# A 2x2 average pool limited by the DMA engines: quarter loads from GpSimd flagged as single packets, and 32 KB store descriptors

## The chip, the cores and the metric

The kernel runs on one core of a Trainium2 chip. The metric is the device time of one execution in microseconds (us). The granted clock was 1.0, and the program used this one core. A time quoted as a median comes from four to seven executions of one kernel.

## The reference, cut to what matters

```python
x = np.random.randn(32, 128, 256, 256).astype(np.float32)   # 1073.7 MB
# kernel_size = 2, stride = 2
output[:, :, i, j] = np.mean(x[:, :, 2*i:2*i+2, 2*j:2*j+2], axis=(2, 3))   # 268.4 MB
```

Every input byte is read once and every output byte written once: 1342.2 MB in all. One output row of 128 values needs two input rows of 256 values. The kernel calls such a pair of rows a unit; there are 4096 units for each of the 128 partitions.

## The kernel before

A tile is 32 units for each partition, which is 64 KB a partition and 8.39 MB in all. There are two buffers for tiles. For each tile, one transfer on SP's queue loads it, VectorE adds twice, ScalarE multiplies by 0.25, and one transfer on ACT's queue stores 16 KB a partition.

```python
sbuf = ctx.enter_context(tc.tile_pool(name="sbuf", bufs=2))
...
for parts in plan:                      # 126 whole tiles, then smaller parts
    in_tile = sbuf.tile([P, G_MAIN, s * w], mybir.dt.float32, name="in_tile")
    ...
        nc.sync.dma_start(out=it, in_=xt)
        nc.vector.tensor_add(out=it[:, :, 0:w], in0=it[:, :, 0:w], in1=...)       # L87
        col_sum = sbuf.tile([P, G_MAIN, w_out], mybir.dt.float32, name="col_sum", bufs=3)
        nc.vector.tensor_add(out=col_sum[:, :g], in0=it[:, :, 0:wu:s], in1=...)   # L96
        nc.scalar.mul(out=col_sum[:, :g], in_=col_sum[:, :g], mul=inv)
        nc.scalar.dma_start(out=ot, in_=col_sum[:, :g])
```

## Time and profile before

The median is 3106.5 us (3106.2 to 3106.7).

| part of a full tile | time |
|---|---|
| VectorE, two additions | 8.69 + 4.42 us |
| ScalarE, one multiplication | 3.62 us |
| from one tile to the next | 24.18 us |
| load issued ahead of the previous tile's landing | about 11 us |

These lines are from the page of the kernel before: the span, the busy times, the data rate in 40 equal slices of the span, and the two DMA queues (packets, MB, share of 16 engines' span).

```profile
span 3104.8 us, 1126 instructions
DVE 1681.4 (54%) x272; ACT 465.8 (15%) x137; POOL 0.2 (0%) x4
DMA  9999999999999999999999999999999999999999
GB/s 418 436 439 425 436 439 425 436 438 429 433 439 430 431 439 434 427 439 435 426 438 436 427 437 436 428 436 437 427 436 437 428 436 437 429 435 437 432 431 396
q1 hardware_dynamic: 19584, 1073.75, 79.8%
q10 hardware_dynamic: 19584, 268.44, 20.2%
```

The DMA engines are full from end to end, and the two queues share them almost exactly as they share the bytes, 4:1. VectorE is busy about half of the time. Its timeline (start, duration, what, and in brackets the idle time before it and what ended that) shows how even the pace is:

```profile
1494.01 8.69 DVE L87 TENSOR_TENSOR in_tile<-in_tile 128x8192 f32<-128x8192 f32 x1 [10.97 <-DMA in_tile<-in_x_dram]
1502.79 4.42 DVE L96 TENSOR_TENSOR col_sum<-in_tile 128x4096 f32<-128x4096 f32 x1
1518.19 8.69 DVE L87 TENSOR_TENSOR in_tile<-in_tile 128x8192 f32<-128x8192 f32 x1 [10.97 <-DMA in_tile<-in_x_dram]
1526.97 4.42 DVE L96 TENSOR_TENSOR col_sum<-in_tile 128x4096 f32<-128x4096 f32 x1
1542.66 8.69 DVE L87 TENSOR_TENSOR in_tile<-in_tile 128x8192 f32<-128x8192 f32 x1 [11.27 <-DMA in_tile<-in_x_dram]
```

Read the bracket as a reserve. With two buffers, the load of tile i+2 is issued when VectorE is done with tile i. VectorE then idles until tile i+1 lands, and that idle time is how far ahead the load of tile i+2 was queued. I call it the lead of the loads: 11 us here.

The trace also holds one record for each DMA descriptor (queue, start, duration, size; the page calls them packets). It does not name the engine, so I assigned records to 16 lanes by matching each start to the end of an earlier record. Lanes can be mixed up when two ends coincide, but the pattern repeats. One lane of the steady state, from that list and not from a view of the profile (L64:2418 is a load descriptor of 64 KB that took 2418 ns, S16 a store descriptor of 16 KB, Ls and Ss are the 4-byte completions):

```
before   L64:2418 S16:611 Ls:9 Ss:9 L64:2418 S16:611 L64:2418 S16:611 L64:2418 S16:611 L64:2418 ...
```

Loads and stores alternate one for one, and nearly every descriptor takes the same time. The two sizes fit 8.6 ns + bytes / 27.2 GB/s. I call this the unobstructed time and what a record takes beyond it its stretch. Over the whole run the stretch is 1.4 us (summed over all records, divided by 16 engines).

### The profile page before, as it was taken

To read this page: it belongs to the slowest core of one execution; us is meant where nothing else is said; L and a number is where in the kernel's file an instruction comes from. 1 tells how busy PE (TensorE), PEld (TensorE's weight loads), DVE (VectorE), ACT (ScalarE), POOL (GpSimd) and SP (SyncE) were. 2 spreads that over 40 slices of the span, in tenths; PEclk is the share of its full clock that TensorE was granted. 3 is DMA by queue.
4 is the path that set the end of the run, shared out by engine and by line. 5 is a ranking of instruction groups with operands and counts; after the bars stand their busy time and mean duration, and the time that the engine had idled before them with its cause. 6 is when DMAs were issued, how large, how long until landed. Compare 5 with 4: busy or idle time off the path is not lost. (4 is left out here: it accounts for less than half of the span.)

```text
span 3104.8 us, 1126 instructions
## 1 busy us (share of the span) xinstructions
DVE 1681.4 (54%) x272; ACT 465.8 (15%) x137; POOL 0.2 (0%) x4
## 2 busy tenths in 40 slices
DVE  4555555555555555555555555555555555555556
ACT  1111111111111111111111111111111111111112
POOL 0000000000000000000000000000000000000000
DMA  9999999999999999999999999999999999999999
GB/s 418 436 439 425 436 439 425 436 438 429 433 439 430 431 439 434 427 439 435 426 438 436 427 437 436 428 436 437 427 436 437 428 436 437 429 435 437 432 431 396
DMA packets 39176, 1342.26 MB, mean 432 GB/s; under 512 B 4352, under 2 KB 4736, under 8 KB 5888
## 3 DMA queue, kind: packets, MB, share of 16 engines
q1 hardware_dynamic: 19584, 1073.75, 79.8%
q10 hardware_dynamic: 19584, 268.44, 20.2%
q14 instruction: 8, 0.07, 0.0%
HBM read 1073.74 MB, written 268.44 MB: 432 GB/s over the span
## 5 line engine op out<-in xcount | busy, mean ns | idle before, releaser
L87 DVE TENSOR_TENSOR in_tile<-in_tile 128x8192 f32<-128x8192 f32 (+4 forms) x136 | 1113.9, 8190 | 1406.7 <-DMA in_tile<-in_x_dram 1406.7
L108 ACT ACTIVATE col_sum<-col_sum 128x4096 f32<-128x4096 f32 (+4 forms) x136 | 464.5, 3415 | 2635.9 <-DVE col_sum L96 2635.9
L96 DVE TENSOR_TENSOR col_sum<-in_tile 128x4096 f32<-128x4096 f32 (+4 forms) x136 | 567.8, 4175 | 13.9 <-DMA out_dram<-col_sum 1.8
L108 ACT ACT_TABLE_LOAD x1 | 1.3, 1283 | 0.7 <-PEq L190 0.7
L190 POOL MEMSET const-bfloat16-1.0<- 128x1 bf16 x1 | 0.1, 102 | 0.0
L190 POOL MEMSET const-uint8-127<- 128x1 uint8 x1 | 0.1, 102 | 0.0
L190 POOL MEMSET const-float32-0.0<- 128x1 f32 x1 | 0.1, 99 | 0.2 <-issue 0.2
L190 POOL MEMSET const-float32-1.0<- 128x1 f32 x1 | 0.1, 99 | 0.0
## 6 DMA issues: line engine op xcount, KB each, us to landing
out_dram<-col_sum ACTq DMA_DIRECT2D x126, 2048.0 KB, 31.6
in_tile<-in_x_dram SPq DMA_DIRECT2D x5, 2048.0 KB, 27.5
in_tile<-in_x_dram SPq DMA_DIRECT2D x1, 4096.0 KB, 25.5
out_dram<-col_sum ACTq DMA_DIRECT2D x5, 512.0 KB, 12.0
in_tile<-in_x_dram SPq DMA_DIRECT2D x126, 35.1
out_dram<-col_sum ACTq DMA_DIRECT2D x1, 1024.0 KB, 12.7
in_tile<-in_x_dram SPq DMA_DIRECT2D x1, 1024.0 KB, 16.2
in_tile<-in_x_dram SPq DMA_DIRECT2D x1, 512.0 KB, 16.9
```

The lines of the kernel that those rows point to most:

```text
L87: nc.vector.tensor_add(out=it[:, :, 0:w], in0=it[:, :, 0:w], in1=it[:, :, di * w : (di + 1) * w],)
L96: nc.vector.tensor_add(out=col_sum[:, :g], in0=it[:, :, 0:wu:s], in1=it[:, :, 1 : wu + 1 : s],)
L108: nc.scalar.mul(out=col_sum[:, :g], in_=col_sum[:, :g], mul=inv)
L190: nc = _bacc.Bacc("TRN2", target_bir_lowering=False, num_devices=1)
```

## The change

The intent is to halve the number of turns between loads and stores while keeping 4:1. Each tile is loaded in four transfers of every fourth partition, in which an engine has two descriptors of 64 KB, flagged to go as a single packet of 128 KB. Two tiles are stored by one transfer with 32 KB descriptors. The loads move to GpSimd's queue, and the tail is cut differently.

```diff
-            nc.sync.dma_start(out=it, in_=xt)
+    def load(it, xt):
+        for q in range(4):
+            nc.gpsimd.dma_start(out=it[q::4], in_=xt[q::4], single_packet=True)
...
+    while left >= 4 * TILE:                       # TILE = 32
+        xt, ot = block(r0, 2 * TILE)              # 64 units a partition, 128 KB in HBM
+        res = out_pool.tile([P, 2 * TILE, w_out], f32, name="res")      # two of these
+        for a in (0, TILE):
+            it = in_pool.tile([P, TILE, 2 * w], f32, name="in_tile")    # two of these
+            load(it, xt[:, a : a + TILE])
+            pool(it, res[:, a : a + TILE])        # the same two additions and the mul
+        nc.scalar.dma_start(out=ot, in_=res)
...
+    # tail: one tile whose store is held back to GpSimd's queue, then parts of 16, 8, 4, 4 units
```

## The prediction

> **What bounds it now.** The DMA engines. The page's slice row shows them 90% busy or more in all 40 slices; its queue table gives loads 79.8% of 16 engines' span and stores 20.2%. 1342.26 MB in a 3104.8 us span is 432 GB/s. VectorE is busy 54%, ScalarE 15%. In the timeline a full tile takes 8.69 + 4.43 us on VectorE and 3.62 us on ScalarE, but tiles follow each other every 24.17 to 24.19 us (a few 24.4 to 24.9), and VectorE idles about 11 us before each, waiting for the load. A tile moves 8.39 MB in and 2.10 MB out: 10.486 MB / 24.175 us = 433.7 GB/s. Loads alone, before the first store, ran at 8.39 MB / 19.32 us = 434.2 GB/s.
>
> The Trainium skill, "DMA: Bandwidth & Descriptors", section "Where 436 GB/s comes from", gives 435.2 GB/s as the SBUF-side ceiling. The trace agrees to 0.4%. At that figure the bytes take 3084 us (estimate), so the kernel has about 22 us to give: some 10 in steady state (128 tiles x 0.08 us), 2 to 4 at the start, some 7 in the tail (the windows view shows 405 GB/s in the last 105 us).
>
> **What the change does.** Loads move from SP's queue to GpSimd's. A 64 KB packet per partition becomes one packet of two partitions (128 KB) per engine; store packets go from 16 to 32 KB. Load packet to store packet stays 4:1, as are the bytes, so alternating packet by packet keeps the queues in balance, with half the switches. If the 0.08 us per tile is paid per packet, half returns: about 5 us. Against that each tile has four load completions instead of one; I allow 0 to 0.1 us a tile, up to 12 us lost. Compute per tile is unchanged. GpSimd has no other work, and a load is issued about 11 us before the previous one lands, which hides slower issue. The start loses about 1 us to GpSimd's issue path. The tail has fewer pieces (16, 8, 4, 4 units, one held-back 2 MB store filling the DMA engines): 0 to 4 us gained; VectorE may wait there for the last 4 MB store to free its buffer.
>
> Nearly all of this is on the critical path, but the sums are tiny: -5 +3 +1 -3, about -4 us.
>
> **Prediction.** 3102 us, range 3089 to 3122. Faster by over 2% would need about 441 GB/s, above anything the trace shows for loads: 3%. Within 2%: 90%. Slower by over 2%: 7%.
>
> **What would show each step.** Right: the DMA row still full, GpSimd's queue near 80% of the engines; load packets per byte about half; VectorE's rhythm 24.1 to 24.25 us per tile, still about 11 us idle per tile for the load; compute busy times unchanged; last 100 us above 405 GB/s. Wrong: a rhythm well over 24.3 us with VectorE waiting longer for loads, or VectorE waiting for stores (two result buffers too few).
>
> **What would make it wrong.** (1) Engine-to-partition assignment. The skill's "SBUF — State Buffer", section "Door 1", maps each group of partitions to one of 16 ports. If 32 partitions taken every fourth are dealt two neighbours to an engine (0 and 4, 8 and 12), two engines meet on one port and loads slow a lot; if each engine keeps its own port's partitions, nothing is lost. No trace here shows which; this is most of the 7%. (2) Completions costing far more on GpSimd's queue. (3) Stores starved behind 128 KB packets, so VectorE waits for a free result buffer. (4) A gain, if overlapping packets let an engine exceed its 27 GB/s.

## More of the kernel before

The experiments ran in five groups, each on a chip of its own with the kernel before beside it. Some comparisons go across groups; the kernel before's medians in the five agree within 0.2 us.

## The result, and the profile after

The changed kernel takes 3203.8 us (median of 4, 3195.2 to 3224.6) against 3106.5 us: slower, ratio 1.032 (1.029 to 1.036). A ratio here is the mean time of one kernel's runs over that of the other's of the same rounds, so it is not quite the ratio of the medians. All four runs counted; their scatter of nearly 1% is new, as the kernel before scatters by 0.02%.

The same lines of the page after the change; its profiled run took 3195.2 us:

```profile
span 3193.5 us, 1676 instructions
DVE 1679.7 (53%) x262; ACT 464.5 (15%) x132; POOL 275.4 (9%) x529
DMA  9999999999999999999999999999999999999999
GB/s 418 426 413 420 420 420 419 419 420 422 417 424 410 417 419 416 424 420 414 421 421 423 420 428 423 419 422 424 424 425 428 424 419 430 417 421 427 422 423 395
q0 software_dynamic: 25296, 1075.87, 80.1%
q10 hardware_dynamic: 9648, 266.34, 19.7%
```

Compute is the same, the engines still look full, and yet they moved 420 GB/s instead of 432 on average. VectorE waits longer for loads. Its waits before and after (engine and line, what it waited for, us in total, times, longest us):

```profile
DVE in_tile L87 <- DMA in_tile<-in_x_dram: 1406.7, 133, 22.7
DVE in_tile L61 <- DMA in_tile<-in_x_dram: 1498.0, 129, 23.6
```

So the transfers themselves take longer. The packet count of the load queue is a first hint: 25296 less the completions (525 transfers x 16 = 8400) leaves 16896 packets of data, as many as one for each partition and transfer, so no data was recorded in 128 KB pieces. VectorE's timeline shows the second hint:

```profile
1495.37 8.69 DVE L61 TENSOR_TENSOR in_tile<-in_tile 128x8192 f32<-128x8192 f32 x1 [17.11 <-DMA in_tile<-in_x_dram]
1504.10 4.42 DVE L62 TENSOR_TENSOR res<-in_tile 128x4096 f32<-128x4096 f32 x1
1514.90 8.69 DVE L61 TENSOR_TENSOR in_tile<-in_tile 128x8192 f32<-128x8192 f32 x1 [6.38 <-DMA in_tile<-in_x_dram]
1523.68 4.43 DVE L62 TENSOR_TENSOR res<-in_tile 128x4096 f32<-128x4096 f32 x1
1545.39 8.69 DVE L61 TENSOR_TENSOR in_tile<-in_tile 128x8192 f32<-128x8192 f32 x1 [17.29 <-DMA in_tile<-in_x_dram]
1554.12 4.43 DVE L62 TENSOR_TENSOR res<-in_tile 128x4096 f32<-128x4096 f32 x1
1564.82 8.69 DVE L61 TENSOR_TENSOR in_tile<-in_tile 128x8192 f32<-128x8192 f32 x1 [6.27 <-DMA in_tile<-in_x_dram]
```

The even rhythm of 24.18 us has become a pair: about 19.4 us, then about 30.4 us, and the lead of the loads falls to 6.3 us in every second tile. A tile in 19.35 us is 434 GB/s of loads alone: no store ran there. A pair takes about 49.7 us where two tiles took 48.36, and 1.35 us x 63 pairs = 85 us, nearly the whole loss.

The lane of one engine shows why there are pairs:

```
after    ... L64:2418 L64:2418 Ls:9 L64:2713 L64:3220 S32:1213 Ls:9 S32:1213 L64:2620 S32:1213 L64:2418
         S32:1213 Ls:9 S32:1213 L64:2418 S32:1213 L64:2418 S32:1213 Ls:9 S32:1213 L64:3185 Ss:9 L64:2418 ...
```

Loads and stores still take turns descriptor by descriptor, now 64 KB against 32 KB, and a load's completion takes a turn too, so that each two load descriptors (128 KB) meet three stores (96 KB). The stores of a pair are used up in some 22 us. Then the store queue is empty for 27 us, until the next pair is done and the stores start again.

The lost time sits at these restarts and ends. The windows view of the changed kernel over one restart (from, to, length, busy time of VectorE, ScalarE and GpSimd, granted clock, DMA share, GB/s) shows loads alone, the restart, the mixed stretch, the end of the stores, and loads alone again:

```profile
1495.40:1511.00 15.60, 13.09 (x2) 2.44 (x1) 2.10 (x4) 1.00 1.00 433
1511.00:1519.00 8.00, 4.10 (x1) 1.17 (x1) 0.00 (x0) 1.00 0.96 360
1519.00:1534.00 15.00, 9.02 (x2) 3.62 (x1) 2.10 (x4) 1.00 1.02 437
1534.00:1543.00 9.00, 0.00 (x0) 0.00 (x0) 0.00 (x0) 1.00 1.04 415
1543.00:1560.00 17.00, 13.12 (x2) 1.42 (x1) 1.16 (x3) 1.00 1.00 432
```

In such short windows a descriptor that straddles an edge blurs the rate, but the records agree: stretched load descriptors of up to 3.4 us lie just before and at the first stores, and a second group lies around the last ones. In between, with stores and loads mixed, descriptors are back at 2418 and 1213 ns. So here 32 KB stores beside 64 KB loads cost nothing once they run.

Summed over all descriptor records (neighbours on an engine overlap by 4 ns, which is taken off), the two spans divide like this:

| us, mean of 16 engines | before | after | difference |
|---|---|---|---|
| unobstructed time of all data descriptors | 3094.3 | 3091.7 | -2.6 |
| stretch | 1.4 | 84.3 | +82.9 |
| rest (start, tail, idle, completions) | 9.1 | 17.5 | +8.4 |
| span | 3104.8 | 3193.5 | +88.7 |

Fewer descriptors did save 2.6 us. Stretch gave it all back thirty times over. Of the 8.4 us in the rest, some 6 us are gaps in mid-run, in which fewer than 16 descriptors were under way. The profiled run was the fastest of the four; the median run lost 97 us.

### The profile page after: what moved, and what is told of

The parts are those of the page before. It is cut to its first block, busy times and chain, and to the rows that moved or that the text cites. A ratio compares the mean times of both kernels' runs of the same rounds, so it can differ in the third digit from the quotient of the medians.

```text
span 3193.5 us, 1676 instructions
## 1 busy us (share of the span) xinstructions
DVE 1679.7 (53%) x262; ACT 464.5 (15%) x132; POOL 275.4 (9%) x529
## 3 DMA queue, kind: packets, MB, share of 16 engines
q0 software_dynamic: 25296, 1075.87, 80.1%
## 4 chain that ended last, share of the span: by engine, by line
DMA 69%; DVE 26%; POOL 3%; issue 1%; DVEq 0%; ACT 0%; ACTq 0%; PEldq 0%
DMA in_tile<-in_x_dram 69%; DVE in_tile L61 17%; DVE res L62 9%; POOL in_tile L58 3%; ACT res L63 0%; DVEq L61 0%; DVEq L62 0%; ACTq L112 0%; PEldq L204 0%
## 5 line engine op out<-in xcount | busy, mean ns | idle before, releaser
L61 DVE TENSOR_TENSOR in_tile<-in_tile 128x8192 f32<-128x8192 f32 (+1 forms) x131 | 1113.1, 8497 | 1498.1 <-DMA in_tile<-in_x_dram 1498.0
L63 ACT ACTIVATE res<-res 128x4096 f32<-128x4096 f32 (+1 forms) x131 | 463.2, 3538 | 2723.0 <-DVE res L62 2722.5
L62 DVE TENSOR_TENSOR res<-in_tile 128x4096 f32<-128x4096 f32 (+1 forms) x131 | 566.7, 4327 | 9.5 <-DMA in_tile<-in_x_dram 1.3
L58 POOL DMA_DIRECT2D in_tile<-in_x_dram x524 | 274.7, 527 | 2902.1 <-DVE res L62 2849.0
```

The lines of the kernel that those rows point to most:

```text
L58: nc.gpsimd.dma_start(out=it[q::4], in_=xt[q::4], single_packet=True)
L62: nc.vector.tensor_add(out=dst, in0=it[:, :, 0:w:2], in1=it[:, :, 1:w:2])
L63: nc.scalar.mul(out=dst, in_=dst, mul=0.25)
```

## The experiments

All kernels gave correct results. Each is the changed kernel with the edit shown (e18 builds on e3), so they share its tail and its paired layout. Each was run four times, with seven runs of before beside it, whose medians were 3106.3 to 3106.4 us. Where an edit has one mul for a pair, the mul for each tile is left out. "Stretch" and "dry" (how long the store queue is empty before a restart) come from the descriptor records of the profiled run. Counted from the last store on any engine to the next first one, "dry" comes out up to 3 us shorter. Stretch is put down to a restart or to the end of the stores, whichever is nearer in time. Losses of about 1% below are clear of the noise: e2's ratio of 1.013 has an interval of 1.011 to 1.015.

**The first four** take the change apart. Theory A was: the mismatch of turns makes the stores stop and go, and each restart costs. Its rivals were GpSimd's loads (B), the 128 KB row pitch in HBM that pairing brings (C), and 32 KB descriptors as such (D).

```diff
 # e1_pool_16k: one store per tile
             pool(it, res[:, a : a + TILE])
-        nc.scalar.dma_start(out=ot, in_=res)
+            nc.scalar.dma_start(out=ot[:, a : a + TILE], in_=res[:, a : a + TILE])
 # e2_sp_32k: the load of before
-        for q in range(4):
-            nc.gpsimd.dma_start(out=it[q::4], in_=xt[q::4], single_packet=True)
+        nc.sync.dma_start(out=it, in_=xt)
 # e3_sp_16k: both of these
 # e4_no_single
-            nc.gpsimd.dma_start(out=it[q::4], in_=xt[q::4], single_packet=True)
+            nc.gpsimd.dma_start(out=it[q::4], in_=xt[q::4])
```

> The changed kernel with one edit: each tile is stored by itself, so store descriptors are 16 KB again. Theory A (stop and go: the engines alternate load and store descriptor by descriptor, 64 KB against 32 KB, so the stores run at twice the share of the bytes, run dry and start again once per pair of tiles, and each stop and start costs the engines about 1.35 us): back to 3095-3110 us, tiles every 24.1-24.3 us, load descriptors at 2418 ns throughout. Theory B (GpSimd's loads: four quarters, their completions or descriptor rings, slow mixed traffic): stays near 3190-3205. Theory C (the 128 KB pitch of the rows in HBM that the pairing of tiles brings): stays near 3190-3205. Theory D (a 32 KB store descriptor is slow in itself): 3095-3110, like A.

> The changed kernel with the loads of before (one transfer of 128 partitions per tile on SP's queue), 32 KB stores kept. A: as slow as the changed kernel, 3180-3210 us, tiles alternating near 19.35 and 30.3 us. B: 3095-3110. C and D: 3180-3210.

> The changed kernel with both undone: SP loads and 16 KB stores, but the paired layout (128 KB pitch) and the new tail kept. A, B, D: 3095-3108 us. C: 3180-3205.

> The changed kernel without the single-packet flag. A: the descriptors were dealt one by one even with the flag, so no change, 3190-3215 us. If the flag itself costs the time (it holds an engine through two descriptors): clearly faster than the changed kernel. If the flag does hold two load descriptors together in part, dropping it makes the alternation worse: over 3215.

| | median us | ratio to before | stretch us | dry us |
|---|---|---|---|---|
| e1_pool_16k | 3110.7 | 1.001 | 2.9 | 8 |
| e2_sp_32k | 3150.3 | 1.013 | 50.4 | 22 |
| e3_sp_16k | 3105.2 | 1.000 | 1.5 | never |
| e4_no_single | 3199.7 | 1.030 | 99.1 | 27 |

Going back to 16 KB stores removes the loss (e1, e3), so neither GpSimd's quarters alone nor the row pitch is the cause: C falls. The flag makes no difference that stands out of the scatter (e4, 3180 to 3222 us, against 3195 to 3225 with it), and the lane of e4 shows the same order of descriptors. But e2 was a miss for every theory. SP's loads with 32 KB stores lose 44 us, only half, and the stretch lies almost wholly at the restarts (47.9 of 50.4 us); the stretch at the ends, 45 us in the changed kernel, is gone. These lines of e2's VectorE timeline show the pairs again:

```profile
1512.31 8.69 DVE L60 TENSOR_TENSOR in_tile<-in_tile 128x8192 f32<-128x8192 f32 x1 [16.20 <-DMA in_tile<-in_x_dram]
1531.65 8.69 DVE L60 TENSOR_TENSOR in_tile<-in_tile 128x8192 f32<-128x8192 f32 x1 [6.19 <-DMA in_tile<-in_x_dram]
1561.34 8.69 DVE L60 TENSOR_TENSOR in_tile<-in_tile 128x8192 f32<-128x8192 f32 x1 [16.48 <-DMA in_tile<-in_x_dram]
```

And e1 hurts theory A as it stood: its stores run dry for about 8 us in every tile, 125 times, and nearly all of its load descriptors take 2418 ns. A restart alone costs little.

**The next four** ask what a restart needs in order to cost, and whose the other half is.

```diff
 # e5_sp_l32_s16: 32 KB loads, and both 16 KB stores issued together at the pair's end
+        for b in range(0, g, 16):
+            nc.sync.dma_start(out=it[:, b:e], in_=xt[:, b:e])     # e = min(g, b + 16)
-        nc.scalar.dma_start(out=ot, in_=res)
+        nc.scalar.mul(out=res, in_=res, mul=0.25)                 # one mul for the pair
+        for a in (0, TILE):
+            nc.scalar.dma_start(out=ot[:, a : a + TILE], in_=res[:, a : a + TILE])
 # e7_sp_l64_s16_pair: those stores, and nc.sync.dma_start(out=it, in_=xt)
 # e6_two_load_queues: quarters 0 and 2 on nc.gpsimd as before, 1 and 3 on nc.sync
 # e8_pool_one
+        nc.gpsimd.dma_start(out=it, in_=xt, single_packet=True)   # no quarters
```

> Loads on SP's queue as two transfers of 32 KB descriptors per tile; the two stores of 16 KB descriptors of a pair issued together at the pair's end. 32:16 keeps the 2:1 alternation of the changed kernel, so the store queue should be empty for about 20 us of each 48 us, with no 32 KB store descriptor anywhere. Theory A2 (what costs is a long stretch without stores, then a restart; a short one, as in e1_pool_16k, costs nothing): 0.4-0.8 us per pair lost, 3130-3165 us. Theory D2 (what costs is the size of the 32 KB store descriptors at the restart): 3105-3120 us, the surplus over 3105 being the per-descriptor cost of twice the descriptors.

> The changed kernel, but two of the four quarter loads go to SP's queue and two stay on GpSimd's. With three queues dealt one descriptor each, a turn is 64 + 64 KB of loads to 32 KB of stores, 4:1 like the bytes, so stores should hardly run dry although they still are 32 KB descriptors issued once per pair. A2: most of the loss gone, 3100-3130 us, store queue empty under 10 us per pair. D2: about 3150 or more.

> Loads of before on SP's queue (64 KB descriptors), two stores of 16 KB descriptors issued together at the pair's end: stores are issued as rarely as in the changed kernel, but 64:16 makes them last the whole 48 us. A2 and D2: 3103-3112 us. If issuing stores once per pair is what costs: 3140 or more.

> The changed kernel with one GpSimd load of 128 partitions per tile in place of the four quarters; 32 KB stores kept. The completions of the four quarters took turns of their own in the alternation, 3 store turns to 128 KB of loads. If that (or the quarters) is the part of the loss that SP's loads did not have: like e2_sp_32k, 3140-3160 us. If it is GpSimd's queue as such: 3190-3215 us.

| | median us | ratio to before | stretch us | dry us |
|---|---|---|---|---|
| e5_sp_l32_s16 | 3114.8 | 1.003 | 3.3 | 21 |
| e6_two_load_queues | 3143.0 | 1.012 | 31.1 | 13 |
| e7_sp_l64_s16_pair | 3105.7 | 1.000 | 1.7 | 5 |
| e8_pool_one | 3148.5 | 1.014 | 45.6 | 23 |

e7 clears the rarer issue of stores. e8 equals e2, so GpSimd's queue as such is innocent, and cutting a tile into quarters is the other half of the loss: 3203.8 - 3148.5 = 55 us. e5 restarts 62 times after 21 us dry and loses only 8 us: 4.4 us are the unobstructed time of twice the load descriptors, 2 us are stretch, and the remainder lies outside the data descriptors. So the length of the dry spell is not it either. With one mul for the pair, e5 issues its stores later after a load than e2 does (7.1 against 3.7 us), but e11 below is as late (7.5 us) and loses 36 us, so lateness does not explain e5. e6 was meant to bring back 4:1 and did not: the completions of its quarters took turns, and the stores still ran dry. Its 3143 us lies between its two ranges.

**The third four** separate the size of a descriptor from the bytes of a turn, and quarters from GpSimd.

```diff
 # e9_sp_quarters_32k:  nc.gpsimd -> nc.sync for the four quarters, no flag
 # e10_sp_l32_s32: the 32 KB loads of e5, the 32 KB store of the changed kernel
 # e11_sp_l64_s16x2: SP's whole loads; the pair's stores on two queues
+        nc.scalar.dma_start(out=ot[:, :TILE], in_=res[:, :TILE])
+        nc.gpsimd.dma_start(out=ot[:, TILE:], in_=res[:, TILE:])
 # e12_halves_two_queues
+        nc.sync.dma_start(out=it[0::2], in_=xt[0::2])
+        nc.gpsimd.dma_start(out=it[1::2], in_=xt[1::2])
```

> The changed kernel with its four quarter loads per tile issued from SP's queue instead of GpSimd's; 32 KB stores kept. e8_pool_one showed that GpSimd's queue with whole-tile loads is no slower than SP's with them. If cutting a tile into quarters is the second half of the loss: like the changed kernel, 3185-3215 us, with stretched descriptors at the end of the stores too. If it takes quarters and GpSimd together: about 3150.

> SP loads of 32 KB descriptors, 32 KB stores once per pair. e5_sp_l32_s16 (32 against 16) lost nothing at its restarts. If the size of the store descriptor sets the cost of a restart: 0.5-0.8 us per pair, 3145-3165 us. If it takes a 64 KB load descriptor as well: 3108-3120 us.

> SP loads of 64 KB descriptors; the two 16 KB stores of a pair are issued together from two queues (ACT and GpSimd), so a turn is 64 KB of loads to 16 + 16 KB of stores: the stores run dry for about 20 us per pair as in e2_sp_32k, with no 32 KB descriptor. If the cost of a restart comes from the 32 KB descriptor: 3103-3112 us. If it comes from restarting at double share beside 64 KB loads: 3130-3160 us.

> The changed kernel with a tile's load as two transfers of every second partition, one on SP's queue and one on GpSimd's: 64 + 64 KB of loads per 32 KB store, and only one completion turn for each, so the stores last nearly the whole 48 us. If a 32 KB store stream that never stops costs nothing: 3100-3115 us, stores dry under 6 us per pair. If the restarts still come and cost: 3130-3150 us.

| | median us | ratio to before | stretch us | dry us |
|---|---|---|---|---|
| e9_sp_quarters_32k | 3235.9 | 1.042 | 108.4 | 28 |
| e10_sp_l32_s32 | 3136.1 | 1.010 | 27.1 | 31 |
| e11_sp_l64_s16x2 | 3142.8 | 1.011 | 34.8 | 22 |
| e12_halves_two_queues | 3140.0 | unsettled | 13.2 | 7 |

Quarters on SP's queue are slower still than on GpSimd's (e9 - e2 = 86 us), so the quarters, not the queue, cost that half. e11 has no 32 KB descriptor and loses like e2: two 16 KB descriptors in a turn do the same as one of 32 KB, and D falls. e10 missed its 3145 us but lost more than the 3108 to 3120 of its rival: 21 us over e5, which has the same loads and half the store turn. Its stretch is about half of e2's (27.1 against 50.4 us) with the same stores, so the size of the load descriptors counts as well. e12 came out at 3109.1, 3120.1, 3159.8 and 3173.4 us; by the rule of 1.5% above the fastest, two of those count as slow, though one core ran at full clock in all of them. Its ratio of 1.003 rests on the other two, so I draw nothing from it.

**The last six** follow what was open: why a turn of 16 KB is free and one of 32 KB is not.

```diff
 # e13_pool_quarters_s16_pair: the changed kernel's loads, the stores of e5
 # e14_sp_l64_s32x2: SP's whole loads, one mul per pair, the pair's store by partitions
+        nc.scalar.dma_start(out=ot[0::2], in_=res[0::2])
+        nc.gpsimd.dma_start(out=ot[1::2], in_=res[1::2])
 # e15_sp_l64_s24: the same, but 24 KB and 8 KB descriptors
+        nc.scalar.dma_start(out=ot[:, :48], in_=res[:, :48])
+        nc.scalar.dma_start(out=ot[:, 48:], in_=res[:, 48:])
 # e16_four_small_buffers: SP's whole loads, half tiles in four buffers, store per four
-TILE = 32
+TILE = 16
-    in_pool = ctx.enter_context(tc.tile_pool(name="inp", bufs=2))
+    in_pool = ctx.enter_context(tc.tile_pool(name="inp", bufs=4))
+        for a in range(0, 4 * TILE, TILE):
```

> The changed kernel with the two stores of a pair as 16 KB descriptors, issued together at the pair's end: GpSimd quarters and 64 KB loads stay, and the stores are dry for 12-17 us per pair. If the bytes of a store turn set the cost (16 KB free, 32 KB not): 3105-3115 us. If dry spells of over 10 us beside 64 KB loads set it: 3130-3160 us.

> SP loads of 64 KB descriptors; the pair's store split by even and odd partitions over the ACT and GpSimd queues, two 32 KB descriptors per turn: 64 KB of stores per 64 KB of loads. If the bytes of a store turn set the cost: about twice the loss of e2_sp_32k or more, 3180-3230 us. If each restart costs the same whatever the turn: 3140-3160 us.

> SP loads of 64 KB descriptors; the pair's store as one transfer of 24 KB and one of 8 KB descriptors, issued together. If the bytes of a store turn set the cost: between e7 (16 KB, 3105) and e2 (32 KB, 3150), 3112-3140 us. Like e2 (over 3140) if any restart with more than 16 KB costs the same.

> SP loads of 32 KB descriptors in four buffers of half a tile each (same memory), so that loads are queued further ahead, and 32 KB stores per 64 units as in e10_sp_l32_s32, whose restarts cost about 0.4 us each (3136 us; without them about 3115). If a short queue of loads is what makes a restart cost: 3112-3120 us. If not: 3130-3145 us.

| | median us | ratio to before | stretch us | dry us |
|---|---|---|---|---|
| e13_pool_quarters_s16_pair | 3118.4 | 1.004 | 10.5 | 12 |
| e14_sp_l64_s32x2 | 3305.3 | 1.064 | 158.1 | 31 |
| e15_sp_l64_s24 | 3106.5 | 1.000 | 1.7 | 5 |
| e16_four_small_buffers | 3115.3 | 1.003 | 4.6 | 31 |

e13 came out 3 us above its range for 16 KB turns, and only 0.8 of its 10.5 us of stretch lie at restarts. e14 doubles the turn to 64 KB and loses 199 us, four and a half times e2's loss and above both of its ranges. That fits a cost that grows with the bytes of a store turn. But e14 also splits the store by partitions, which no run tests apart, 44 of its 158 us of stretch lie at the ends of the stores, and some 40 us more are gaps in which engines had nothing to do. e15 turned out not to test what it was for: after the eight turns of 24 KB come eight of 8 KB, so its stores hardly stopped; it only shows that a 24 KB turn is harmless in a stream that runs on.

e16 is the run that points to a missing condition. It has e10's descriptors, 32 KB against 32 KB, restarts 63 times after 31 us dry, and loses little: 3115.3 us, like e5 with its 16 KB turns. What differs most is how many loads are queued. These two lines, from the DMA views of e10 and then e16, give the median from a load's issue to its landing in the last column:

```profile
in_tile<-in_x_dram SPq DMA_DIRECT2D x255, 4096.0 KB, 26.3
```

```profile
in_tile<-in_x_dram SPq DMA_DIRECT2D x255, 4096.0 KB, 41.7
```

Four half buffers hold the same bytes as two whole ones, but a half buffer comes free sooner, so loads are queued 41.7 instead of 26.3 us before they land. Counted from the issues and the records, the loads issued and not yet moved never fell below 8.0 MB in e16's steady state; in e10 they fell to 1.5 MB. Two more runs, the last of the eighteen, put this to the test.

```diff
 # e17_changed_four_buffers: the changed kernel itself with e16's TILE = 16 and bufs=4
 # e18_late_loads: e3 with the second addition done twice, so buffers come free 4.4 us later
         nc.vector.tensor_add(out=dst, in0=it[:, :, 0:w:2], in1=it[:, :, 1:w:2])
+        nc.vector.tensor_add(out=dst, in0=it[:, :, 0:w:2], in1=it[:, :, 1:w:2])
```

> The changed kernel, GpSimd quarters, flag and 32 KB stores and all, with four load buffers of half a tile in place of two of a tile (same memory). If its whole loss comes from restarts of the stores met with too few loads queued: 3113-3128 us (about 10 us over 3105 for twice the load descriptors, some more for the quarters). If quarters cost in another way: 3150 or more.

> e3_sp_16k (SP loads of 64 KB, 16 KB store per tile) with the second addition of each tile done twice, same result: VectorE holds each buffer 4.4 us longer, so a load is issued about 6.6 us before the previous one lands, like the shortest in the changed kernel (6.2), but the stores never stop. If a short queue of loads costs by itself: 0.5 us a tile or more, 3160-3200 us. If it takes a restart of the stores as well: 3104-3112 us.

| | median us | ratio to before | stretch us | dry us |
|---|---|---|---|---|
| e17_changed_four_buffers | 3150.3 | 1.014 | 33.5 | 33 |
| e18_late_loads | 3111.1 | 1.002 | 3.6 | never |

In e18 the lead is 6.5 us, as short as the changed kernel's shortest, and yet nothing is lost in the steady state:

```profile
2972.30 8.69 DVE L60 TENSOR_TENSOR in_tile<-in_tile 128x8192 f32<-128x8192 f32 x1 [6.56 <-DMA in_tile<-in_x_dram]
2996.47 8.69 DVE L60 TENSOR_TENSOR in_tile<-in_tile 128x8192 f32<-128x8192 f32 x1 [6.50 <-DMA in_tile<-in_x_dram]
3020.65 8.69 DVE L60 TENSOR_TENSOR in_tile<-in_tile 128x8192 f32<-128x8192 f32 x1 [6.56 <-DMA in_tile<-in_x_dram]
```

The starts lie 24.17 and 24.18 us apart. Of its 6 us over e3, 2 are stretch (3.6 against 1.5 us) and most of the rest lies in the tail, where the doubled additions follow the last loads: in the last 110 us, the engines' gaps sum to 8.0 us, against 4.5 in e3. So a short queue of loads alone is harmless, too. The reading that fits is that it takes both: a store stream that restarts with 32 KB a turn or more, and few loads queued.

e17 missed: it gives back 53 of the changed kernel's 97 us, not all. Even these 53 do not speak for depth, because half tiles also halve the load descriptors to 32 KB, as in e10, and the queue did not get deeper. This is visible in its waits (same columns as above):

```profile
POOL in_tile L58 <- DMA in_tile<-in_x_dram: 2520.2, 999, 8.5
```

GpSimd waits 999 times for an earlier load to land before it issues the next quarter, which it did 9 times in the changed kernel. Its loads are queued only 23.2 us ahead (median from issue to landing), so e17 never had e16's depth; the loads issued and not yet moved came to 7.9 MB at most. Whether quarters would be free with that depth, no run shows.

No version beats the kernel before by a margin worth having. e3 (3105.2 us) and e7 (3105.7 us) are within 0.05% of it.

## Why the prediction was wrong

The prediction gave 3102 us, range 3089 to 3122, and 7% to a slowdown of over 2%. It came to 3203.8 us.

- **What bounds the kernel: right.** The DMA engines did before and do after; compute is off the path in both. The ceiling of 435.2 GB/s that the Trainium skill gives in "DMA: Bandwidth & Descriptors", section "Where 436 GB/s comes from", agrees with 434 GB/s in the load-only tiles of both kernels.
- **"Load packet to store packet stays 4:1 ... so alternating packet by packet keeps the queues in balance, with half the switches": this is the step that failed.** It took the 128 KB packet from the flag and the intent. The records show turns of one 64 KB descriptor against one of 32 KB, and the run without the flag has the same order and a time within the scatter. The stores get 1 byte for each 1.3 to 2 bytes of loads while they last, instead of 1 for 4, and then run dry for 27 us of 50. The prediction looked at whether stores might starve; they were overfed.
- **"Half returns: about 5 us": right in kind, 2.6 us in size**, by the sum over descriptors. It was buried under 82.9 us of stretch, a term the prediction did not have.
- **"A load is issued about 11 us before the previous one lands": it became 6.3 us in every second tile**, because the uneven stores make every second tile land after 19.4 us while VectorE still needs 13.1. e10 against e16 suggests, but does not prove, that the depth of the load queue bears on what a restart costs.
- **"0 to 0.1 us a tile" for four completions: mis-sized.** Quarters cost 55 us over whole-tile loads (0.43 us a tile), as part of the stop and go. Beside 16 KB stores the same quarters cost 5.5 us (e1 - e3) or 12.7 us (e13 - e7). The fear that this was GpSimd's doing fell: SP's quarters are slower (e9).
- **Port conflicts (risk 1): not seen.** The map in the Trainium skill's "SBUF — State Buffer", section "Door 1", would have let two engines meet on a port if neighbours in a quarter had gone to one engine. Tiles of quarter loads with no store beside them landed in 19.35 us, as fast as whole-tile loads, so no sign of it is there.
- **Compute busy times unchanged, DMA row still full: right**, and a warning: the DMA row reads 9 everywhere in both pages. A busy share cannot tell a descriptor that moves from one that is stretched. The prediction's own sign of being wrong, a rhythm over 24.3 us with longer waits for loads, did appear: 24.8 us a tile on average.

What stays open is what holds a descriptor up inside an engine. The runs show two conditions: the stores restart (in e3, e7 and e15 they run on almost without a break, and nothing is lost), and they do so with 32 KB or more a turn (e10 against e5; in e11 two descriptors of 16 KB count like one of 32). The third, a short queue of loads, rests on e16 alone. e16 also changed where a restart falls relative to the issue of a load, and halved the size of VectorE's instructions, so depth itself is the best reading, not the only one. No run settles whether 32 KB stores are free when the turns fit the bytes: e6 ran dry all the same, and e12's times spread. Why quarters add stretch at the ends of the stores (45 of 84 us in the changed kernel, 2 in e8) is open, too; e14 has as much there without quarter loads.

## What to carry to other kernels

When two DMA queues share the engines, compare the bytes of one turn of each with the bytes that each must move, counting turns by descriptors (and completions) in the trace, not by what a flag promises. Where the turns fitted the bytes in these runs, both streams ran on almost without a break, and stores of 24 KB (e15), loads of 64 KB (e7) or a late issue (e18) did no harm. Where they did not fit, one stream stopped and went, and its restarts could cost far more than fewer descriptors saved (83 against 2.6 us). If a stream must stop and go, turns of 16 KB cost little here (e5); queueing more loads is worth a try (e16).

## What the Trainium skill lacked or had wrong

- "DMA: Bandwidth & Descriptors", section "Queues, rings and completion order", says that an engine takes turns between queues and "drains a whole packet (≈9-17 descriptors typical, spec ceiling ≤64)" first. The turns are there, but with descriptors this large the typical count did not hold: each turn was one data descriptor, 64 KB against 16 or 32 KB. The single-packet flag on two descriptors did not change the order, nor the time beyond the scatter (3203.8 us with it, 3199.7 without). No page says what the flag does.
- The same section does not say that a completion takes a turn: in the changed kernel each pair of 64 KB loads met three stores of 32 KB, not two.
- The same page, "Rules for kernel authors", says that spreading DMAs over several queues "Doesn't help". It also changes the shares: the same loads with the pair's 16 KB stores on one queue took 3105.7 us (e7) and on two queues 3142.8 us (e11).
- No page has the cost of stopping and restarting a store stream beside loads: 0.7 us a pair in e2 (44 us in 63 pairs), 3.2 us with a turn of 64 KB (e14, its store split by partitions too), next to nothing with 16 KB (e5) or with four half-tile buffers (e16).
- The same rules advise one transfer of 128 partitions over two of partition halves because these serialize. The runs show no gain from quarters either, and add what they can cost: 55 us on GpSimd's queue, 86 us on SP's, beside 32 KB stores, and 5.5 to 12.7 us beside 16 KB stores.
